# Head gates by seven block products, kept in DRAM; heads in two lanes; the second projection's weight sums all in layer 2

## The chip, the cores and the metric

The kernel runs on one core of a Trainium2 chip. Its time is the device time of one execution in microseconds (us). The kernel before was timed three times: 1390.17, 1392.6 and 1392.98 us, with a median of 1392.6 us. One more execution was profiled; the rows below come from it, and it took 1390.15 us.

## What is computed

512 tokens of width 2048 pass through two layers in float32. Layer 1 (cut from the reference):

```python
q, k, v, g_att, z, xbc, dt_raw = split(x @ w_in)       # q,k,v,g_att,z: 512 x 1024 each
o = rms_norm(diff_attention(q, k, v, lam), subln_g) * (1.0 - lam_init)   # 8 heads of 128
y_att = o.reshape(s, 1024) * silu(g_att)
y = ssd_chunked(...) + d_skip * xs                      # 16 state-space heads of 64
y = rms_norm(y * silu(z)) * ssm_norm_g                  # in two groups of 512
x = layer_norm(alpha * x + concat([y_att, y]) @ w_out)
```

Layer 2 projects x to a value and a gate path of 2048 each, pools the values over causal windows of 2, 4, 8 and 16 tokens in four groups, maps each group by a 512 x 512 matrix, multiplies by the gates, and sends that through a second output projection and a layer norm.

## The kernel before

**Products.** Each float32 product is three matmuls (`mm3`, L106 to L108): high part by high part, and the two cross terms. Weights come in "units" of 128 x 1024 float32 (512 KB). `unit` (L119) loads one by a DMA on SyncE's queue into a `raw` buffer (three in turn); ScalarE casts it to `hi` (L116), and VectorE subtracts to get `lo` (L117). A block of 128 output columns for all 512 tokens (`ws_block`) takes two units and 48 matmuls.

**Seven block products.** The z gate and both output projections are computed as 2 x 2 block matrices with seven block products in place of eight (`prod`, four units and 48 matmuls for one block product of z). This needs sums of weight blocks. `presum` (L240) makes them by DMA alone on GpSimd's queue: it copies blocks into an SBUF buffer, adds others by accumulating DMAs (L236), and writes each partial sum to DRAM (L238). Each step waits for the one before in its buffer. Two such chains (a pair) run at a time, in two lanes `sums2`. Layer 1 uses the buffers `pre` and `pre3`. In layer 2 each chain has a buffer `pre2` that shares its place (`h1` or `l1`) with a later tile: `yr2`, the third pooling group's result, takes `h1`, and `yr3` takes `l1`. GpSimd's queue also holds the small powers of the norms (`power`, L231), and it works strictly in order.

**Lanes.** A lane is a list of Python generators. Work with its own chain of waits is written as steps with `yield us`. Each `mm3` tells all lanes how much matmul time has been written since, and a lane whose wait is over writes its next step. So the order on TensorE is fixed when the program is built: small matmuls stand between large ones, and TensorE works through them in that order, waiting where an operand is late.

**Order of layer 1.** B, C, x and v projections with the state-space steps; the z gate; then for each head h `k_block`, `q_block` and `g_block` of the head before (48 matmuls each). `attention(h)` is pushed to `lane`: for each of four query blocks i `scores(i)` (into psc, with max, exp and the combination on VectorE and ScalarE), `turn(i)` (transposes into pat, copied to aT) and `values(i)` (into pav). After `values(3)` come four squares of pav on ScalarE (L706), two small VectorE operations, the power on GpSimd (L231) and the scaling `o` on VectorE (L712). Then `pot` transposes o (L719), and VectorE multiplies it by gain and gate into yTa (L722). After the heads follows the first output projection: Y = a11 by w (`pY`), which runs beside the last head's attention, then V (`pZ`), which needs yTa of all heads, then the products with sums.

**Layer 2.** For each group `vblock`, `pool_block`, `gblock` and the group map (`pgr`); VectorE forms y (L972), and ScalarE writes `yr` from it (L974). After the residual has been moved to DRAM (`x1d`, L916), three pairs of wo2 chains follow in GpSimd's queue; the first pair of all wo2 sums was made in layer 1.

Of the kernel before, what the change touches and what calls it, by code (L numbers as in the profile page):

```python
# [16 lines left out]
P = 128  # L17
T = 512
# [70 lines left out]
def hybrid_trunk(ctx: ExitStack, tc: tile.TileContext, xT, xtok, wa, wg, wz, wo1, wo2, prm, con, lnp, out, dbg=None):  # L89
# [135 lines left out]
    tsz, ts1, ts2 = {}, {}, {}  # L225
# [44 lines left out]
    with ExitStack() as l1:  # L270
# [14 lines left out]
        with ExitStack() as sd:  # L285
# [235 lines left out]
        with tc.tile_pool(name="zs", bufs=1) as zq:  # L521
# [46 lines left out]
            for i in range(2):  # L568
                c = zq.tile([P, T], F32, tag="zc", name="zc", bufs=2)
                nc.scalar.copy(c, Wz[i])  # L570
                nc.vector.tensor_tensor(c, c, Yz[i], ALU.add)
                th = zq.tile([P, 2, T], F32, tag="zo", name="zt", bufs=2)
                z_gate(2 + i, 0, c, th[:, 0])
                nc.vector.tensor_tensor(c22[i], c22[i], Yz[i], ALU.subtract)
                z_gate(2 + i, 1, c22[i], th[:, 1])
            for l in sums2:
                l.off = False
# [5 lines left out]
        ssq = at.tile([P, 8], F32, name="ssq")  # L583

        def ssm_norm(g):
# [11 lines left out]
            for c in range(4):  # L597
# [5 lines left out]
                yield 1.5  # L603

# [29 lines left out]

        gts = {}

        def g_block(h):
            pg = bank("mm", "pgt")
            ws_block(pg, next_units(2), xh, xl)
            gt = a2.tile([P, T], F32, tag="gt", name="gt")  # L640
            gate(gt, pg)
            gts[h] = gt

        def attention(h, kS, qH, qL):
# [32 lines left out]
            def values(i):  # L677
# [3 lines left out]
            yield 2.5  # L681
            scores(0)
            yield 3.5
            scores(1)
            yield 3.5
            turn(0)
            scores(2)
            pav = bank("aux", "pav")
            yield 2.5
            values(0)  # L690
            turn(1)
            yield 3.0
            values(1)
            scores(3)
            yield 2.5
            turn(2)
            yield 3.0
            values(2)
            yield 1.5
            turn(3)  # L700
            yield 3.0
            values(3)
            ss = a2.tile([P, 2, NT], F32, tag="ss", name="ss")
            for i in range(NT):
                junk = a2.tile([P, T], F32, tag="gth", name="junk")
                nc.scalar.activation(junk[:, :P], pav[:, ts(i)], AF.Square, accum_out=ss[:, 0, i:i + 1])  # L706
            s0 = st[:, 1, :, 0]
            nc.vector.scalar_tensor_tensor(ss[:, 1], in0=s0, scalar=EPS, in1=s0, op0=ALU.mult, op1=ALU.mult)
            nc.vector.scalar_tensor_tensor(ss[:, 0], in0=ss[:, 0], scalar=1.0 / P, in1=ss[:, 1], op0=ALU.mult, op1=ALU.add)
            power(ss[:, 0], 4)  # L710
            o = a2.tile([P, NT, P], F32, tag="o", name="o")
            nc.vector.tensor_tensor(o, pav.rearrange("p (i e) -> p i e", i=NT),  # L712
                                    ss[:, 0].unsqueeze(2).broadcast_to([P, NT, P]), ALU.mult)
            yield 5.5
            while h not in gts:
                yield 0.5
            pt = bank("aux", "pot")
            for i in range(NT):
                nc.tensor.transpose(pt[:, ts(i)], o[:, i], ident)  # L719
            if yTa[0] is None:  # L720
                yTa[0] = keep.tile([P, HEADS, T], F32, tag="y", name="yTa")
            nc.vector.scalar_tensor_tensor(yTa[0][:, h], in0=pt, scalar=subg, in1=gts[h], op0=ALU.mult, op1=ALU.mult)  # L722
# [41 lines left out]
        lane.flush()  # L764
        eight(a12, lambda u: yA[:, u:u + 2, H0], (6,))
# [107 lines left out]
    with ExitStack() as l2:  # L873
# [27 lines left out]
        with ExitStack() as mix:  # L901
# [18 lines left out]
            for g, w in enumerate(WINDOWS):  # L920
# [54 lines left out]
                if g == 0:  # L975
# [13 lines left out]
                    for i in range(2, 8):  # L989
                        sums2[i % 2].push(presum(wo2, ts2, i // 4, i % 4, stage2(i % 2), 10.0))  # L990
# [136 lines left out]
def _pack(inputs):  # L1127
# [17 lines left out]
    for h in range(HEADS):  # L1145
        ua += ws(w1, 1024 + P * h) + ws(w1, P * h)
        if h > 0:
            ua += ws(w1, 3072 + P * (h - 1))
    ua += ws(w1, 3072 + P * (HEADS - 1))
# [11 lines left out]
    sz = w1[:, 4096:5120].reshape(2, 4, 2, P, 1, 2, 512).transpose(4, 0, 5, 1, 3, 2, 6).reshape(16, P, 1024)  # L1161
# [27 lines left out]
    return {"xT": xT, "xtok": x.reshape(NT, P, D), "wa": wa, "wg": wg, "wz": sz, "wo1": so1, "wo2": so2, "prm": prm, "con": con, "lnp": lnp}  # L1189
# [18 lines left out]
```

## Time and profile before

| | |
|---|---|
| median of three runs | 1392.6 us (1390.17 to 1392.98) |
| profiled execution | 1390.15 us, span 1388.3 us |
| TensorE busy | 1372.6 us, 99% of the span, 6653 matmuls |
| VectorE, ScalarE, GpSimd busy | 870.9, 591.0, 189.1 us |
| mean granted TensorE clock | 0.997 |
| moved by DMA | 304.82 MB, mean 220 GB/s |

The time of the profiled execution is 1.85 us above its span. A share of busy time alone does not tell which engine sets the time; the waits and the rows of a stretch do. "TensorE busy" counts matmuls from start to modelled end, and they overlap, so durations of matmuls are read from the distance of their starts.

### The profile page before, as it was taken

The numbers are of one execution on the slowest core, as the hardware profiler recorded it, in microseconds if no ns is written. First come the engines' busy times: TensorE is split into PE (matmuls) and PEld (weight loads), VectorE is DVE, ScalarE is ACT, GpSimd is POOL, SyncE is SP. The second block draws the span as 40 slices with busy tenths as digits, with TensorE's granted clock in tenths as the row PEclk, the third lists the DMA queues.
The fourth block names the chain that finished last, engine by engine and source line by source line (L and its number), as shares of the span: only waits on it lengthen the run. The fifth ranks groups of instructions, "written<-read, shape, count | busy, mean of one in ns | idle before, by whom it ended". The sixth has DMA issues, their size and how long they took to land.

```text
span 1388.3 us, 17493 instructions
## 1 busy us (share of the span) xinstructions
PE 1372.6 (99%) x6653; PEld 1156.6 (83%) x6653; DVE 870.9 (63%) x1251; ACT 591.0 (43%) x960; POOL 189.1 (14%) x285
## 2 busy tenths in 40 slices
PE   9999999999999999999999999999999999999996
PEld 7988899888888888888888889888888888888875
DVE  7755764577645555556796897855345256466766
ACT  5232443456554444445544556333232232345443
POOL 0222220000221122200000000222221000200003
PEclk9999999999999999999999999999999999999998
DMA  8899996467777698832586556699999423566776
GB/s 303 270 313 303 276 265 182 123 238 247 244 198 232 198 265 245 239 123 76 174 294 193 176 179 189 220 319 293 311 289 289 135 91 95 181 202 195 246 247 122
DMA packets 88036, 304.82 MB, mean 220 GB/s; under 512 B 10000, under 2 KB 10128, under 8 KB 87568
## 3 DMA queue, kind: packets, MB, share of 16 engines
q1 hardware_dynamic: 52704, 177.86, 38.5%
q0 software_dynamic: 35248, 125.85, 33.5%
q8 instruction: 52, 0.85, 0.3%
q14 instruction: 32, 0.26, 0.1%
HBM read 249.14 MB, written 57.67 MB: 221 GB/s over the span
## 4 chain that ended last, share of the span: by engine, by line
PE 91%; DVE 4%; DMA 2%; issue 1%; ACT 1%; POOL 1%; DVEq 0%; ACTq 0%; POOLq 0%; SPq 0%
PE pg L106 6%; PE pg L107 6%; PE pg L108 6%; PE pY L107 4%; PE pY L108 4%; PE pY L106 4%; PE pv L107 4%; PE pv L106 4%; PE pv L108 4%; PE pZ L107 3%; PE pZ L106 3%; PE pZ L108 3%; PE pgt L108 2%; PE pxs L106 2%; PE pgt L106 2%; PE pxs L108 2%
## 5 line engine op out<-in xcount | busy, mean ns | idle before, releaser
L117 DVE TENSOR_TENSOR lo<-raw,hi 128x1024 fp32r<-128x1024 f32 (+3 forms) x314 | 373.5, 1190 | 326.3 <-ACT hi L116 323.3
L116 ACT CAST hi<-raw 128x1024 fp32r<-128x1024 f32 (+3 forms) x314 | 321.4, 1024 | 526.0 <-PE pY L108 83.6
L107 PE MATMUL pv<-x1l,hi 128*128 128x512 f32 (+1 forms) x320 | 110.9, 347 | 0.0
L106 PE MATMUL pv<-x1h,hi 128*128 128x512 f32 (+1 forms) x320 | 110.9, 347 | 0.0
L108 PE MATMUL pv<-x1h,lo 128*128 128x512 f32 (+1 forms) x320 | 110.7, 347 | 0.0
L106 PE MATMUL pg<-x1h,hi 128*128 128x512 f32 x256 | 99.6, 389 | 0.0
L107 PE MATMUL pg<-x1l,hi 128*128 128x512 f32 x256 | 99.6, 389 | 0.0
L108 PE MATMUL pg<-x1h,lo 128*128 128x512 f32 x256 | 99.6, 389 | 0.0
L238 POOL DMA_DIRECT2D t<-pre x80 | 44.7, 560 | 209.7 <-DMA pre<-in_wo 159.3
L236 POOL DMA_DIRECT2D pre<-in_wo x64 | 56.4, 956 | 96.1 <-DMA t<-pre 52.9
L107 PEld LDWEIGHTS pv<-x1l,hi 128*128 128x128 f32 x320 | 60.5, 189 | 7.6
L106 PEld LDWEIGHTS pv<-x1h,hi 128*128 128x128 f32 x320 | 60.5, 189 | 7.6
L108 PEld LDWEIGHTS pv<-x1h,lo 128*128 128x128 f32 x320 | 60.4, 189 | 7.5
L106 PE MATMUL pg<-hi,xh 128*128 128x346 f32 (+1 forms) x192 | 63.6, 332 | 0.0
L107 PE MATMUL pg<-lo,xh 128*128 128x346 f32 (+1 forms) x192 | 61.8, 322 | 0.0
L108 PE MATMUL pg<-hi,xl 128*128 128x346 f32 (+1 forms) x192 | 61.5, 320 | 0.0
L659 ACT ACTIVATE pm<-psc,st 128x128 f32<-128x128 f32 (+3 forms) x64 | 33.1, 523 | 61.0 <-DVE st L656 60.9
L108 PEld LDWEIGHTS pg<-x1h,lo 128*128 128x128 f32 x256 | 48.1, 188 | 10.0
L106 PEld LDWEIGHTS pg<-x1h,hi 128*128 128x128 f32 x256 | 48.1, 188 | 10.0
L107 PEld LDWEIGHTS pg<-x1l,hi 128*128 128x128 f32 x256 | 48.1, 188 | 9.9
L106 PE MATMUL pq<-xh,hi 128*128 128x512 f32 x128 | 51.9, 405 | 0.0
L106 PE MATMUL pgt<-xh,hi 128*128 128x512 f32 x128 | 51.8, 405 | 0.0
(366 smaller groups left out, 3259.8 us busy)
## 6 DMA issues: line engine op xcount, KB each, us to landing
raw<-in_wa SPq DMA_DIRECT2D x150, 512.0 KB, 5.0
pre<-in_wo POOLq DMA_DIRECT2D x96, 512.0 KB, 8.1
t<-pre POOLq DMA_DIRECT2D x80, 512.0 KB, 6.0
raw<-t SPq DMA_DIRECT2D x80, 512.0 KB, 4.2
raw<-in_wo SPq DMA_DIRECT2D x48, 512.0 KB, 3.7
pre<-in_wz POOLq DMA_DIRECT2D x24, 512.0 KB, 8.6
raw<-in_wz SPq DMA_DIRECT2D x12, 512.0 KB, 3.7
raw<-in_wg SPq DMA_DIRECT2D x16, 346.0 KB, 6.5
```

The costliest lines, as they stand in the source:

```text
L106: nc.tensor.matmul(o, sh, mh, start=start, stop=False, skip_group_check=more)
L107: nc.tensor.matmul(o, sh, ml, start=False, stop=False, skip_group_check=more)
L108: nc.tensor.matmul(o, sl, mh, start=False, stop=stop, skip_group_check=more)
L116: nc.scalar.copy(hi, src)
L117: nc.vector.tensor_tensor(lo, src, hi.bitcast(F32), ALU.subtract)
L236: nc.gpsimd.dma_start(dst, src, accum_op=ALU.add)
L238: nc.gpsimd.dma_start(dst, src)
L659: nc.scalar.activation(pm[:, m, :ke], pt[:, m, :ke], AF.Exp, bias=st[:, 0, i, m:m + 1], scale=1.0, accum_out=st[:, 1, i, m:m + 1])
```

## The change

- The 16 weight blocks of the heads' gates become an input of their own, `wga`. After z, 28 units and 336 matmuls compute the gates by seven block products, with four more chains in `presum`. `g_gate` writes each gate tile to a DRAM tensor `gd` by GpSimd's queue (8 writes of 256 KB).
- The eight `g_block`s (384 matmuls) go. Each head loads its gate from `gd` on SyncE's queue (`gt`) and multiplies o by it on VectorE before the transposes; ScalarE scales pot into yTa.
- Even heads go to `lane`, odd heads to `lane2`, so that two heads interleave. `busy` keeps the second from taking pav before the first has formed o. Steps are paced at 1.1 times their figures, for the last head at 0.6.
- In layer 1 the chains are wz 4, wga 4 and wo1 8, with shorter waits; the two wo2 chains go to layer 2, where four pairs now follow each other in place of three.

```diff
-            for w, tsum, n, pace in ((wz, tsz, 4, 7.0), (wo1, ts1, 8, 8.0), (wo2, ts2, 2, 8.0)):
+            for w, tsum, n, pace in ((wz, tsz, 4, 5.6), (wga, tsg, 4, 5.6), (wo1, ts1, 8, 6.0)):
...
+            def g_gate(t, j, c, th):
+                gate(th, c)
+                nc.gpsimd.dma_start(gd[:, t, j * 512:(j + 1) * 512], th)
...
+            gd = dram.tile([P, NT, 1024], F32, name="gd")
+            Yg = pair("mm")
+            for ch in range(4):
+                prod(Yg, xblock(0, H0), unit(wsrc(wga, 0, 0, 0, ch)), ch, True, False)
+            Wg = pair("sc")
+            for ch in range(4):
+                prod(Wg, z3, unit(tsg[3, 0, ch]), ch, True, False)
+            z1 = zsum("z1")
+            fill(z1, 1)
...
-        def g_block(h):
-            pg = bank("mm", "pgt")
-            ws_block(pg, next_units(2), xh, xl)
-            gt = a2.tile([P, T], F32, tag="gt", name="gt")
-            gate(gt, pg)
-            gts[h] = gt
...
+                while busy:
+                    yield 0.5
+                busy.append(h)
+                pav = bank("aux", "pav")
+                gt = a2.tile([P, NT, P], F32, tag="gt", name="gt")
+                nc.sync.dma_start(gt, gd[:, :, ts(h)])
...
+                nc.vector.tensor_tensor(o, o, gt, ALU.mult)
+                busy.remove(h)
+                yield 5.5
+                while len(normed) < 2:
+                    yield 0.5
+                pt = bank("aux", "pot")
...
+                nc.scalar.activation(yTa[0][:, h], pt, AF.Copy, scale=subg)
+
+            for us in steps():
+                yield us * (0.6 if h == HEADS - 1 else 1.1)
...
-            lane.push(attention(h, kS, qH, qL))
-            if h > 0:
-                g_block(h - 1)
-        g_block(HEADS - 1)
+            (lane, lane2)[h % 2].push(attention(h, kS, qH, qL))
...
         lane.flush()
+        lane2.flush()
...
-                    for i in range(2, 8):
-                        sums2[i % 2].push(presum(wo2, ts2, i // 4, i % 4, stage2(i % 2), 10.0))
+                    for i in range(8):
+                        sums2[i % 2].push(presum(wo2, ts2, i // 4, i % 4, stage2(i % 2), 8.0))
```

Three places in the order of instructions. The first is TensorE at the end of the last head's attention, beside the first output projection (pY). Before, from the last `values` (pav) to the first matmul of V (pZ), there are 24 matmuls of pY, of which the first and last rows stand here:

```order
L679 MATMUL pav<-v,aT 128x128 x4
L106 MATMUL pY<-hi,a11h 128x512
L107 MATMUL pY<-lo,a11h 128x512
...
L107 MATMUL pY<-lo,a11h 128x512
L108 MATMUL pY<-hi,a11l 128x512
L719 MATMUL pot<-kc,o 128x128 x4
L106 MATMUL pZ<-hi,a12h 128x512
```

And after the change, at the same place, with every row from pav to pZ:

```order
L728 MATMUL pav<-v,aT 128x128 x4
L106 MATMUL pY<-hi,a11h 128x512
L107 MATMUL pY<-lo,a11h 128x512
L108 MATMUL pY<-hi,a11l 128x512
L106 MATMUL pY<-hi,a11h 128x512
L107 MATMUL pY<-lo,a11h 128x512
L108 MATMUL pY<-hi,a11l 128x512
L106 MATMUL pY<-hi,a11h 128x512
L107 MATMUL pY<-lo,a11h 128x512
L108 MATMUL pY<-hi,a11l 128x512
L776 MATMUL pot<-kc,o 128x128 x4
L106 MATMUL pZ<-hi,a12h 128x512
```

Nine matmuls of pY are left between the last values and the transposes of o. The second place is the same head's scores of the last query block, a little earlier on TensorE. After the change it reads:

```order
L702 MATMUL psc<-kS,qH 128x512
L703 MATMUL psc<-kS,qL 128x512
L721 MATMUL pat<-kc,pm 128x128 x3
...
L776 MATMUL pot<-kc,o 128x128 x4
L728 MATMUL pav<-v,aT 128x128 x3
...
L107 MATMUL pY<-lo,a11h 128x512
L721 MATMUL pat<-kc,pm 128x128 x4
```

Between psc and the four transposes pat stand 14 matmuls of pY and three groups of small ones, one of them (pot) of head 6; before there were 33 matmuls of pY and two groups. The third place is GpSimd's queue in layer 2, at the end of the wo2 chains. Before, the last pair (buffers 9006 and 9009; t_12 and t_13 are sums in DRAM) ends like this, and the next row loads the residual:

```order
L236 DMA pre_9006<-in_wo 128x1024
L236 DMA pre_9009<-in_wo 128x1024
L238 DMA t_12_9235<-pre_9006 128x1024
L238 DMA t_13_9240<-pre_9009 128x1024
L1004 DMA xq_9977<-x1d 128x512 x4
```

After the change one more pair stands between the third and that row; it begins and ends like this:

```order
L238 DMA t_10_9278<-pre_8915 128x1024
L238 DMA t_11_9280<-pre_8918 128x1024
L238 DMA pre_9327<-in_wo 128x1024 x2
L238 DMA pre_9330<-in_wo 128x1024 x2
...
L238 DMA t_12_9378<-pre_9327 128x1024
L236 DMA pre_9330<-in_wo 128x1024
L238 DMA t_13_9390<-pre_9330 128x1024
L1062 DMA xq_10127<-x1d 128x512 x4
```

The pair's instructions are the same in kind and number (4 copies, 6 accumulations, 8 writes), and there is nothing else between the pairs.

## Rows read from the trace of the kernel before

**Rows 1.** The page: busy us and share of each engine, instructions.

```profile
PE 1372.6 (99%) x6653; PEld 1156.6 (83%) x6653; DVE 870.9 (63%) x1251; ACT 591.0 (43%) x960; POOL 189.1 (14%) x285
```

**Rows 2.** Waits (engine, line, waited for: total us, times, longest us).

```profile
PE pbc L306 <- DVE nhalf L174: 1.5, 1, 1.5
PE px L838 <- DVE xp L832: 0.7, 2, 0.5
```

**Rows 3.** Chain that ended last: pot of head 0 and of head 7.

```profile
409.82 0.44 PE pot L719 x4
...
685.00 0.44 PE pot L719 x4
```

**Rows 4.** Windows of z and of a head: us, PE, PEld, DVE, ACT, POOL, clock, DMA share, GB/s.

```profile
285.00:358.00 73.00, 72.85 (x322) 59.74 (x322) 54.25 (x60) 43.90 (x59) 0.78 (x1) 1.00 0.68 227
...
420.00:460.00 40.00, 40.00 (x198) 33.55 (x197) 21.29 (x39) 17.14 (x41) 7.89 (x12) 1.00 0.77 230
```

**Rows 5.** TensorE's timeline (start us, duration us): a k block and the q block behind.

```profile
343.37 0.39 PE L106 MATMUL pk<-xh,hi 128*128 128x512 f32 x1
...
354.25 0.39 PE L106 MATMUL pq<-xh,hi 128*128 128x512 f32 x1
```

**Rows 6.** Groups by form (busy us, mean ns of one | idle before): lo, and o.

```profile
L117 DVE TENSOR_TENSOR lo<-raw,hi 128x1024 fp32r<-128x1024 f32 x286 | 349.6, 1223 | 300.6 <-ACT hi L116 298.0 <-PE pseg L442 0.6
...
L712 DVE TENSOR_TENSOR o<-pav,ss 128x512 f32<-128x512 f32 x8 | 5.5, 692 | 9.6 <-POOL ss L231 9.6
```

**Rows 7.** Timeline of the last head's end, TensorE and VectorE.

```profile
678.49 1.06 PE L679 MATMUL pav<-v,aT 128*128 128x128 f32 x8
...
684.84 0.60 PE L719 MATMUL pot<-kc,o 128*128 128x128 f32 x4
...
682.25 0.69 DVE L712 TENSOR_TENSOR o<-pav,ss 128x512 f32<-128x512 f32 x1 [1.19 <-POOL ss L231]
```

**Rows 8.** Timeline of the last head's scores of query block 3.

```profile
666.46 0.39 PE L654 MATMUL psc<-kS,qL 128*128 128x512 f32 x1
...
675.29 0.60 PE L672 MATMUL pat<-kc,pm 128*128 128x128 f32 x4
...
671.89 0.75 DVE L664 SCALAR_TENSOR_TENSOR pm<-pm,st 128x512 f32<-128x512 f32 x1
```

**Rows 9.** GpSimd's timeline in layer 2: starts of the three pairs, last write from h1.

```profile
908.91 0.55 POOL L238 DMA_DIRECT2D pre<-in_wo  x1
...
973.93 1.06 POOL L238 DMA_DIRECT2D pre<-in_wo  x2 [1.46 <-DMA t<-pre]
...
1026.62 1.06 POOL L238 DMA_DIRECT2D pre<-in_wo  x2 [1.91 <-DMA t<-pre]
...
1073.22 0.56 POOL L238 DMA_DIRECT2D t<-pre  x1 [4.54 <-DMA pre<-in_wo]
```

**Rows 10.** DMA issues near 1026 (copy), 1065 (accumulation), 1073 us (write): KB, us to landing.

```profile
pre<-in_wo POOLq DMA_DIRECT2D x4, 512.0 KB, 6.4
...
pre<-in_wo POOLq DMA_DIRECT2D x1, 512.0 KB, 7.3
...
t<-pre POOLq DMA_DIRECT2D x1, 512.0 KB, 5.4
```

**Rows 11.** ScalarE's timeline in layer 2 around the first write of yr2.

```profile
1114.52 0.72 ACT L974 ACTIVATE yr<-y,osc 128x512 f32<-128x512 f32 x1 [2.19 <-DVE y L972]
1116.27 1.05 ACT L116 CAST hi<-raw 128x1024 fp32r<-128x1024 f32 x1 [1.03 <-PE pgr L107]
...
1127.10 1.05 ACT L116 CAST hi<-raw 128x1024 fp32r<-128x1024 f32 x1 [1.87 <-PE pv L107]
```

**Rows 12.** TensorE's first matmuls, and two windows at the end (columns as in rows 4).

```profile
1.46 3.95 PE L306 MATMUL pbc<-warm 128*128 128x512 f32 x9 [1.46 <-DVE nhalf L174]
...
1376.00:1380.00 4.00, 0.00 (x0) 0.00 (x0) 3.90 (x8) 0.00 (x0) 3.37 (x4) 1.00 1.03 115
1380.00:1384.00 4.00, 0.00 (x0) 0.00 (x0) 3.69 (x6) 0.00 (x0) 0.00 (x0) 0.57 1.03 213
```

More of the change, by code (lines that the diff above doesn't have):

```diff
@@ L88, in hybrid_trunk @@
 @with_exitstack
-def hybrid_trunk(ctx: ExitStack, tc: tile.TileContext, xT, xtok, wa, wg, wz, wo1, wo2, prm, con, lnp, out, dbg=None):
+def hybrid_trunk(ctx: ExitStack, tc: tile.TileContext, xT, xtok, wa, wg, wz, wga, wo1, wo2, prm, con, lnp, out, dbg=None):
     nc = tc.nc
@@ new lines, in hybrid_trunk @@
+            Wg = pair("sc")
[3 more added lines that the diff above has]
+            fill(z1, 1)
+            c22 = [zq.tile([P, T], F32, tag=f"c22{i}", name=f"g22{i}") for i in range(2)]
+            for i in range(2):
+                nc.scalar.activation(c22[i], Wg[i], AF.Copy, scale=-1.0)
+            Vg = pair("mm")
+            for ch in range(4):
+                prod(Vg, xblock(8, H0), unit(wsrc(wga, 1, 0, 0, ch)), ch, True, True)
@@ new lines, in hybrid_trunk @@
+            th = g_th()
+            for i in range(2):
+                c = zq.tile([P, T], F32, tag="zc", name="gc", bufs=2)
+                nc.scalar.copy(c, Vg[i])
+                nc.vector.tensor_tensor(c, c, Yg[i], ALU.add)
+                g_gate(i, 0, c, th[:, i])
+            for ch in range(4):
+                prod(Wg, xblock(8, H1), unit(tsg[4, 0, ch]), ch, False, True)
+            Zg = pair("mm")
+            for ch in range(4):
+                prod(Zg, z1, unit(tsg[1, 0, ch]), ch, True, False)
@@ new lines, in hybrid_trunk @@
+            for i in range(2):
+                nc.vector.tensor_tensor(c22[i], c22[i], Zg[i], ALU.add)
+            for ch in range(4):
+                prod(Yg, z2, unit(tsg[2, 0, ch]), ch, False, True)
+            for i in range(2):
+                th = g_th()
+                c = zq.tile([P, T], F32, tag="zc", name="gc", bufs=2)
+                nc.scalar.copy(c, Wg[i])
+                nc.vector.tensor_tensor(c, c, Yg[i], ALU.add)
+                g_gate(2 + i, 0, c, th[:, 0])
+                nc.vector.tensor_tensor(c22[i], c22[i], Yg[i], ALU.subtract)
+                g_gate(2 + i, 1, c22[i], th[:, 1])
@@ L576, in hybrid_trunk @@
+            for ch in range(4):
+                prod(Zg, z4, unit(wsrc(wga, 1, 1, 0, ch)), ch, False, True)
+            th = g_th()
+            for i in range(2):
+                c = zq.tile([P, T], F32, tag="zc", name="gc", bufs=2)
+                nc.scalar.activation(c, Yg[i], AF.Copy, scale=-1.0)
+                nc.vector.tensor_tensor(c, c, Zg[i], ALU.add)
+                g_gate(i, 1, c, th[:, i])
             for l in sums2:
@@ L583, in hybrid_trunk @@
         ssq = at.tile([P, 8], F32, name="ssq")
+        normed, busy = [], []
         def ssm_norm(g):
@@ L603, in ssm_norm @@
                 yield 1.5
+            normed.append(g)
         for g in range(2):
@@ L675, in turn, with values @@
                 pms[i] = aT
-            def values(i):
+            def values(i, pav):
                 for kb in range(i + 1):
                     nc.tensor.matmul(pav[:, ts(i)], pms[i][:, ts(kb)], v[:, kb, ts(h)], start=(kb == 0), stop=(kb == i))
[L681 to L713, printed above, removed]
@@ L1188, in _pack @@
     lnp = np.stack([f("ln_g"), f("ln_b")], axis=1)
-    return {"xT": xT, "xtok": x.reshape(NT, P, D), "wa": wa, "wg": wg, "wz": sz, "wo1": so1, "wo2": so2, "prm": prm, "con": con, "lnp": lnp}
+    return {"xT": xT, "xtok": x.reshape(NT, P, D), "wa": wa, "wg": wg, "wz": sz, "wga": sg, "wo1": so1, "wo2": so2, "prm": prm, "con": con, "lnp": lnp}
 def kernel(**inputs):
```

57 lines of the change are left out of this document (42 added, 15 removed).

## The prediction

> **What bounds the kernel now.** The page comes first: TensorE is busy for 1372.6 us of a span of 1388.3 [rows 1]. The waits then say whether it ever stands still for an operand: its two longest entries are 1.5 us at the start and 0.7 us in a norm [rows 2]. So the span is the length of what is written on TensorE, and a stretch gets shorter if matmuls leave it, as long as nothing that they hid comes to light. The chain of waits shows the same in the heads: pot of head 0 stands at 409.82 and that of head 7 at 685.00 [rows 3], seven heads at 39.3 us. Last come the windows, to see who has room. In z, VectorE is busy for 54.25 us of 73 and ScalarE for 43.90, while the DMA engines are busy to 0.68; in a head, VectorE has 21.29 us of 40 [rows 4].
>
> **Price of one matmul.** 48 matmuls of a k block lie between 343.37 and 354.25 [rows 5], 0.2267 us each. Durations of single matmuls (0.39 in the same rows) overlap and are not used.
>
> **What is removed.** The change takes out 384 gate matmuls and adds 336; the small ones stay as many. 48 fewer by 0.2267 give **-10.9 us**, if the seven products run without stalls and the shorter heads still cover attention.
>
> *The seven products.* A unit now feeds 12 matmuls (2.7 us) where a gate block's fed 24. The z stage works at just this rate until the first k block at 343.37 [rows 5], and the window that is mostly z has TensorE at 72.85 of 73 us [rows 4]. The added stage is the same code with the same splits, and it has less elementwise work than z (no product with y). Its eight gate writes leave on GpSimd's queue, and the first reader comes a head later. I take 0.
>
> *The heads.* A head had 144 large matmuls, 32.6 us, in a period of 39.3; so 6.7 us are small ones. With 96 the period is 21.8 + 6.7 = 28.5 us. VectorE had about 21 us of work in a head and loses the splits of two units, the gate and the last product, and gains one multiply of 0.69 (as o, [rows 6]); even 21 us would be under three quarters of 28.5. The steps of one head ask for 31 us, times 1.1 is 34.1, and one head's 32 calls of `mm3` tick 32 x 3 x 512/2400 = 20.5. One lane would fall behind by 13.6 a head; two lanes have 41. So the interleaving is needed, and it is enough on paper. The gate load and the pot copy on ScalarE stand where nobody queues behind them for long: 0.
>
> **What comes to light: the end of attention.** V needs the last head, and before, 24 matmuls (5.4 us) of pY stood between its last pav and pot. After the change there are nine, 2.04 us. What must happen in between is read from the trace: pav ends at 678.49 + 1.06 = 679.55, o ends at 682.25 + 0.69 = 682.94 [rows 7], 3.4 us for squares, power and scaling. The new multiply adds 0.69, a hand-over some 0.1: 4.2 - 2.04 = 2.2 us of waiting. A little earlier, 14 matmuls and three small groups, some 4.3 us, separate the last psc from its transposes, where there were 33 and two. The chain of max, exp and combination took from 666.85 (psc's end) to 672.64 (pm's end) [rows 8], 5.8 us. Against 4.3 that is a wait of 1.5; it is 0 if the work of VectorE and ScalarE for the projection that stood among it stands elsewhere. I take 0.8, the middle. Together **+3** (2 to 5.5, the upper end if two splits of 1.2 us [rows 6] also fall into its chain). TensorE has nothing else to do: pZ stands behind pot in its order.
>
> **What comes to light: layer 2.** yr2 lies in h1, the buffer of the even chains. Before, the last write from h1 started at 1073.22 [rows 9] and landed after 5.4 [rows 10], at 1078.6, long before yr2's first write at 1114.52 [rows 11]. Now a fourth chain begins in h1 at 1078.6. How long? Between bounds: the sum of its own landings is 6.4 + 3 x 7.3 + 3 x 5.4 = 44.5 us [rows 10]; the second and third pair took 52.7 (973.93 to 1026.62) and 52.0 [rows 9], the queue's waits for the other chain included. In the new order the even chain's last write stands ahead of the odd chain's last two steps, so I take 48: h1 is free at R = 1126.6 (1123 to 1131). ScalarE is in order, so the cast that ran at 1116.27 stands behind yr2's write until R. Three buffers are in turn and a unit lasts 5.4 us, so this cast fills the unit that TensorE takes up three units on, at 1127.1 (where the cast of 1127.10 finds pv's buffer freed, [rows 11]). It is ready at R + 0.72 (yr) + 1.05 (cast, [rows 11]) + 1.2 (lo, [rows 6]) = R + 3.0, and TensorE waits R - 1124.1, or 2.5 us; with the queue of casts and y behind it I take **+3** (0 to 8).
>
> *In layer 1* the two wo2 chains leave GpSimd's queue, and four wga chains come in. Two wz, two wga and four wo1 pairs of some 52 us [rows 9] now reach into the heads: four wo1 pairs are 208 us beside 228 us of heads. A power of a head's norm can stand behind an accumulation that waits up to 7.3 us; pot follows o's steps after 5.5 x 1.1 us of ticks, which is 6.6 us of matmuls and more, so nearly all is hidden. For this, the chain's last write before the buffers become `sr`, and denser DMA in z I take **+1.5** (0 to 4).
>
> **The sum.** -10.9 + 3 + 3 + 1.5 = -3.4 us. Against the profiled execution that is 1390.15 - 3.4 = 1386.8. That execution is as fast as the fastest of the three shown and 2.45 us under their median; against the median it gives 1389.2, and I say **1389.0**. All terms at their good ends give -8.9, at their bad ends +6.6.
>
> **Rivals.**
> 1. *All is hidden.* If pace 0.6 already lets the last head end early enough and the fourth chain needs only its own landings, -10.9 + 1 leaves 1382.7. For it speaks that TensorE hardly waits anywhere now [rows 2]; against it the nine matmuls against 4.2 us. 0.13.
> 2. *The gain is paid back in full.* The tail at 5.5 and layer 2 at 4 give -10.9 + 9.5 + 1.5 = 0.1, that is 1392.7. For it: every hidden chain was covered by the matmuls that leave. Against: two ends of ranges at once. 0.25.
> 3. *Slower: the fourth chain comes late.* Its place is yr2's first write in ScalarE's order. From R = 1130.5 on the change gains nothing, from 1133 it is slower by 0.2%. At R = 1136 the wait is 12 us, and -10.9 + 3 + 12 + 1.5 = +5.6 gives 1398. For it: the first pair took 65 us (908.91 to 973.93, [rows 9]), which would put R at 1143.6. Against: that pair began right behind the residual's move, the other two did not. 0.15.
> 4. *The heads do not get shorter,* because two heads' steps meet in the single pair of score banks or the lock on pav; 2 us a head bring 16, +12 in all, 1405. Against: VectorE's share and the 41 for 34 ticks. 0.03.
> 5. *The two waits bring TensorE's clock down.* The nine matmuls at the start took 3.95 us where nine at 0.2267 are 2.04 [rows 12], so a return from the lower level costs some 1.9 us; two of them make the sum +0.4, or 1393.0. Against it: at the kernel's end, with no matmul in either window, the granted clock still shows 1.00 from 1376 to 1380, and 0.57 only in the four us behind [rows 12]. My waits are of 3 us at most. In rival 3 it would add another 1.9. 0.04.
>
> The Trainium skill ("TensorE: Matmul & The Clock Gate", section "Why this matters for your kernels") has this as a rule: no idle gaps of TensorE between bursts of matmuls, since the clock falls back to half. The rows at the end show the fall, behind a longer stop than my waits.
>
> **How the numbers follow.** The forecast has 0.40. A measurement of this kernel tells about 0.2%, 2.8 us, from no change. Faster by more are rival 1, some 0.33 of the forecast and 0.01 of rival 2: 0.47. Within it are 0.07 of the forecast, 0.24 of rival 2, 0.01 of rival 3 and rival 5: 0.36. Slower are the rest of rival 3 and rival 4: 0.17. The range runs from rival 1 (1383) to just short of rival 3 (1397); outside are half of rival 1, most of rival 3's late landings, and rival 4, about 2 in 10. The forecast alone would have 1385 to 1392.
>
> **What would show it.** TensorE should have 6605 matmuls. In the waits, pot on o (L776) should show some 2 us and pat on pm up to 1.5, both once, in the last head; a pgr or pv matmul behind yr2 should wait some 3 us on lo, and ScalarE's yr write should name a DMA of `t<-pre` as what it waited for. From pot to pot the heads should average 28.5 us. The prediction is wrong if waits stand in the middle heads or in the gate products, if the fourth pair takes 60 us, or if none of the waits is there.

## The result, and the profile after

The changed kernel takes 1398.45 us (median of 20 runs, 1393.45 to 1405.03); the kernel before, run beside it, takes 1391.2 (1389.8 to 1393.53). The ratio is 1.0055, with a 95% interval of 1.0046 to 1.0064: slower by 0.55%, where 0.2% faster was forecast. The time lies just above the range, near that of rival 3. The profiled execution has a span of 1396.2 us against 1388.3.

First the waits of the kernel after: TensorE's own, those of VectorE and ScalarE that matter (engine, line, waited for: total us, times, longest).

```profile
PE pv L106 <- ACT hi L116: 5.0, 1, 5.0
PE pat L721 <- ACT yTa L779: 2.6, 2, 2.1
PE pot L776 <- DVE o L769: 2.1, 1, 2.1
...
PE pat L721 <- DVE pm L713: 0.5, 1, 0.5
...
DVE o L767 <- POOL ss L231: 12.2, 8, 3.3
...
ACT yr L1032 <- DMA t<-pre: 18.2, 1, 18.2
```

Five waits of TensorE of 0.5 to 5 us have joined those of [rows 2]: one in layer 2 behind yr2, two in middle heads (pat on yTa, 2.1 and 0.5), and two in the last head. The matmuls are 6605, as expected.

Where along the kernel was the time lost? Two places in TensorE's timeline tell: the first matmul of V behind the heads, and the last matmul. Before, V began right behind pot [rows 7]:

```profile
685.19 0.48 PE L106 MATMUL pZ<-hi,a12h 128*128 128x512 f32 x1
...
1375.16 0.39 PE L108 MATMUL pZ<-wl,cl 128*128 128x512 f32 x1
```

After, from the same view:

```profile
685.05 0.63 PE L776 MATMUL pot<-kc,o 128*128 128x128 f32 x4 [2.11 <-DVE o L769]
685.44 0.48 PE L106 MATMUL pZ<-hi,a12h 128*128 128x512 f32 x1
...
1383.07 0.39 PE L108 MATMUL pZ<-wl,cl 128*128 128x512 f32 x1
```

At V the kernel with 48 matmuls fewer is level with the old one (+0.25 us): all of the 10.9 us has been given back in layer 1 already. Its last matmul is at 1383.07 where that of the kernel before was at 1375.16, +7.9 us; so some 7.7 us come after V. The chain of waits after the change, with start, duration and what, shows them at one place in layer 2:

```profile
1121.82 5.67 DMA pre<-in_wo
...
1127.79 2.90 DMA t<-pre
...
1130.95 0.06 ACT yr L1032
...
1131.58 1.04 ACT hi L116
...
1132.65 0.80 PE pv L106
...
1134.71 0.43 PE pv L106
...
1138.37 0.23 PE pv L106
```

The last write of sums from h1 lands at 1130.7; yr2's first write follows at once, behind it the cast that stood in ScalarE's queue, and then TensorE, which had run out of units after 1127.5. That is 5.1 us by the distance of the matmuls. Behind it the matmuls stand 0.43 us apart instead of 0.23, and only from 1138.1 on at the old pitch: TensorE runs at half clock. The windows say the same (us, PE, PEld, DVE, ACT, POOL busy, granted clock, DMA share, GB/s), here and around the wait in the middle head at 495.84:

```profile
494.00:498.00 4.00, 2.16 (x7) 1.81 (x8) 2.23 (x4) 3.00 (x7) 0.57 (x1) 0.79 0.95 228
498.00:502.00 4.00, 4.00 (x17) 3.37 (x16) 1.02 (x2) 0.00 (x0) 1.12 (x2) 0.78 1.01 349
1126.00:1130.00 4.00, 1.70 (x8) 1.08 (x6) 0.00 (x0) 0.00 (x0) 1.23 (x2) 1.00 0.76 275
1130.00:1134.00 4.00, 1.31 (x3) 0.59 (x3) 1.36 (x2) 2.28 (x3) 0.20 (x1) 0.65 0.82 149
1134.00:1138.00 4.00, 4.00 (x10) 3.13 (x11) 2.56 (x4) 2.94 (x4) 0.55 (x1) 0.50 0.77 253
```

The trace's record of the granted clock has 6.8 us at 0.5 in layer 2 (1131.2 to 1138.0) and 3.4 us in the head (496.3 to 499.8). A stretch of 6.8 us at half speed holds 3.4 us of work; some of it was still waiting, and counted by the distance of the matmuls it cost 2.9 us, in the head 1.8. So layer 2 lost 5.1 + 2.9 = 8.0 us.

And the middle head? In these rows of the timelines of GpSimd, VectorE, ScalarE and TensorE the wait at 495.84 is traced back:

```profile
486.25 0.53 POOL L238 DMA_DIRECT2D t<-pre  x1 [3.12 <-DMA pre<-in_wo]
486.80 1.04 POOL L231 TENSOR_TENSOR ss<-ss,nhalf 128x4 f32<-128x4 f32 x1
...
484.44 0.15 DVE L764 SCALAR_TENSOR_TENSOR ss<-ss 128x4 f32<-128x4 f32 x1
487.87 0.69 DVE L767 TENSOR_TENSOR o<-pav,ss 128x512 f32<-128x512 f32 x1 [3.28 <-POOL ss L231]
...
492.92 0.96 DVE L705 TENSOR_REDUCE st<-psc 128x2 f32<-128x768 f32 x1
...
493.97 0.58 ACT L708 ACTIVATE pm<-psc,st 128x384 f32<-128x384 f32 x1 [4.77 <-DVE st L705]
...
495.10 0.69 ACT L779 ACTIVATE yTa<-pot,subg 128x512 f32<-128x512 f32 x1
...
491.07 0.60 PE L776 MATMUL pot<-kc,o 128*128 128x128 f32 x4
...
495.84 0.44 PE L721 MATMUL pat<-kc,pm 128*128 128x128 f32 x2 [2.11 <-ACT yTa L779]
```

VectorE had the mean squares ready at 484.6, but the power stands in GpSimd's queue behind a write of sums that waits for its accumulation to land, and runs at 486.80. VectorE waits in order at o (3.28 us). Behind o stand a split, two parts of kS and the maximum of the *other* head's scores, which comes at 492.92. ScalarE waits for it with the exponentials (4.77 us), and behind these, in its order, stands the copy of pot to yTa, though pot has been done since 491.7. Only two of the small PSUM banks (`aux`) exist; one is the other head's pav, one is pot. So pat of the other head, which needs a bank, waits until 495.8 for that copy.

### The profile page after: what moved, and what is told of

The parts are those of the page before. It is cut to its first block, busy times and chain, and to the rows that moved or that the text cites. A ratio compares the mean times of both kernels' runs of the same rounds, so it can differ in the third digit from the quotient of the medians.

```text
span 1396.2 us, 17592 instructions
## 1 busy us (share of the span) xinstructions
PE 1370.2 (98%) x6605; PEld 1148.7 (82%) x6605; DVE 892.9 (64%) x1275; ACT 613.5 (44%) x990; POOL 220.3 (16%) x333
## 4 chain that ended last, share of the span: by engine, by line
PE 69%; DMA 19%; DVE 4%; issue 4%; POOL 2%; ACT 1%; DVEq 0%; POOLq 0%; ACTq 0%; SPq 0%
DMA pre<-in_wo 11%; DMA t<-pre 6%; PE pY L107 6%; PE pY L106 6%; PE pY L108 6%; PE pg L106 4%; PE pg L107 4%; PE pg L108 4%; PE pZ L107 3%; PE pZ L106 3%; PE pZ L108 3%; PE pxs L106 2%; PE pxs L108 2%; PE pxs L107 2%; PE pv L108 2%
## 5 line engine op out<-in xcount | busy, mean ns | idle before, releaser
L117 DVE TENSOR_TENSOR lo<-raw,hi 128x1024 fp32r<-128x1024 f32 (+3 forms) x326 | 388.3, 1192 | 300.8 <-ACT hi L116 297.2
L116 ACT CAST hi<-raw 128x1024 fp32r<-128x1024 f32 (+3 forms) x326 | 334.3, 1025 | 477.3 <-PE pY L108 94.9
L238 POOL DMA_DIRECT2D t<-pre x96 | 54.4, 567 | 251.1 <-DMA pre<-in_wo 155.4
L108 PEld LDWEIGHTS pg<-x1h,lo 128*128 128x128 f32 x256 | 48.1, 188 | 10.3 <-DVE lo L117 0.4
L106 PE MATMUL pxs<-xh,hi 128*128 128x512 f32 x128 | 51.7, 404 | 0.0
L106 PE MATMUL pk<-xh,hi 128*128 128x512 f32 x128 | 51.3, 401 | 0.0
```

The costliest lines, as they stand in the source:

```text
L106: nc.tensor.matmul(o, sh, mh, start=start, stop=False, skip_group_check=more)
L108: nc.tensor.matmul(o, sl, mh, start=False, stop=stop, skip_group_check=more)
L116: nc.scalar.copy(hi, src)
L117: nc.vector.tensor_tensor(lo, src, hi.bitcast(F32), ALU.subtract)
L238: nc.gpsimd.dma_start(dst, src)
```

## Experiments

Each kernel here was timed beside the kernel before, whose median was 1390.8 to 1391.8 us; the ratios are against it. The changed kernel was not timed again with them, so a difference from its 1398.45 us is good to some 0.6 us, besides its own spread.

**The move of the chains alone.** In the kernel before:

```diff
-            for w, tsum, n, pace in (... (wo1, ts1, 8, 8.0), (wo2, ts2, 2, 8.0)):
+            for w, tsum, n, pace in (... (wo1, ts1, 8, 8.0)):
...
-                    for i in range(2, 8):
-                        sums2[i % 2].push(presum(..., 10.0))
+                    for i in range(8):
+                        sums2[i % 2].push(presum(..., 8.0))
```

> The kernel before, with only the chains of the second projection moved: none in layer 1, four pairs in layer 2 as in the change. Theory (the fourth pair holds yr2's buffer and so ScalarE's queue, and TensorE stands still and then runs for some us at the lower clock level): one wait of about 5 us at a pv matmul on a cast, a stretch of about 7 us at granted clock 0.5 behind it, and +8 us on the kernel before (+4 to +12). Rival (the cost comes from two-lane heads and gates, and layer 2 only looks bad because it starts late there): no wait in layer 2, 0 to +2 us.

It took 1401.78 us, ratio 1.0077 (1.0059 to 1.0096): the kernel before gets 10 us slower by this part alone. But the place was only partly the expected one. Layer 2 has its wait, ScalarE at yr for 14.8 us, but TensorE loses only 1.6 us there in the profiled execution, with no stretch at half clock. The larger loss is a new one in the heads: of the 11.5 us by which its last matmul comes later than before, some 6 lie in the heads, 3.0 in layer 2, and the rest ahead of the heads. The rows (waits, then TensorE's timeline):

```profile
PE pv L106 <- ACT hi L116: 1.6, 1, 1.6
...
DVE sr L759 <- DMA t<-pre: 5.4, 1, 5.4
...
540.78 0.58 PE L653 MATMUL psc<-kS,qH 128*128 128x256 f32 x1 [3.47 <-ACT pm L659]
```

`sr` takes over the chains' buffer for the first projection's differences. With the last chain of layer 1 ending sooner, the scheduler puts this VectorE operation earlier in order, in the middle of a head, and there it waits 5.4 us for the chain's last write (it runs at 538.5; in the kernel before, `sr` first ran at 607.1). From 539.4 on the clock is at half for 6.8 us. So the theory holds for the sign, and for the wait behind the shared buffer; that the size came out near its 8 us is luck, since most of it is from elsewhere. A chain's end has a second reader, whose place in VectorE's order also counts.

**Without the fourth pair in layer 2.** The changed kernel with plain weight blocks in place of the first pair's eight sums; the chains for i = 0 and 1 are left out.

> The changed kernel, with the first pair of the second projection's sums left out (plain weight blocks stand in for its eight sums), so that three pairs are left in layer 2. Theory: yr2's wait and the half-clock stretch in layer 2 are gone, 7.9 us less than the changed kernel, about 1390.5 us, which is the kernel before within 2 us. Rival (layer 2's wait is one of several symptoms of denser DMA traffic): less than 4 us less.

It took 1391.86 us, ratio 1.0005 (0.9994 to 1.0016), 6.6 us under the changed kernel. The wait in layer 2 and the half clock are gone. So this is what makes the change slower; what is left is no slower than before, and no faster. In the profiled execution the middle head waits as long as in the changed kernel, and yet keeps its clock:

```profile
497.17 0.44 PE L721 MATMUL pat<-kc,pm 128*128 128x128 f32 x2 [2.12 <-ACT yTa L779]
...
492.00:496.00 4.00, 3.05 (x17) 2.23 (x15) 3.10 (x5) 0.70 (x3) 1.11 (x2) 1.00 0.94 149
496.00:500.00 4.00, 2.83 (x16) 2.45 (x17) 2.23 (x4) 2.32 (x5) 0.57 (x1) 1.00 1.05 255
```

**All work, but no sharing of h1.** The even chains' long-lived buffer gets 4 KB of its own; the room comes from the residual's two vectors, which move into h1.

```diff
                             a = lp.tile([P, 2, 1024], F32, tag=("h1", "l1")[n], name="pre2")
+                            if n == 0:
+                                return lp.tile([P, 1024], F32, tag="pa", name="pre2t"), a[:, 1]
                             return a[:, 0], a[:, 1]
...
-                    ab = [p2.tile([P, T], F32, tag=f"ab{i}", ...) for i in range(2)]
+                    ab = [abt[:, 2 * (cg % 2) + i] for i in range(2)]
```

> The changed kernel with all its work, but the even chains' long-lived buffer in a place of its own (4 KB a partition, won from the residual's two vectors, which move into h1), so that only the short-lived t3 lies in h1, which yr2 takes. Theory (the sharing of h1, not the DMA traffic, is what layer 2 pays for): no wait of ScalarE on a write of sums at yr2, no wait of TensorE there, no stretch at half clock in layer 2; about 1391.9 us, as with the fourth pair left out (1390 to 1394), 6.6 us less than the changed kernel. Rival (four chains beside layer 2's loads cost by themselves): still 3 us or more over the kernel with the fourth pair left out.

It took 1394.7 us, ratio 1.0028 (1.0019 to 1.0038): 3.7 us under the changed kernel, not 6.6. yr2's wait is gone, four pairs or not. But the edit did more than it was meant to, since the residual's vectors now lie in a place that is free sooner. First, the residual's move ends sooner, and the chains, which stand behind it in GpSimd's queue, begin 21.8 us sooner. GpSimd's timeline has the first copy of the changed kernel, and then the first copy and the even chains' last write of this one:

```profile
911.53 1.60 POOL L238 DMA_DIRECT2D pre<-in_wo  x3
```

```profile
889.77 0.55 POOL L238 DMA_DIRECT2D pre2t<-in_wo  x1
...
1108.67 0.56 POOL L238 DMA_DIRECT2D t<-pre2t  x1 [2.57 <-DMA pre2t<-in_wo]
```

That write lands 5.1 us later, at 1113.8. In the changed kernel ScalarE came to yr2's first write at 1112.7 (18.2 us before 1130.95), and TensorE ran out of work only after 1127.5. So a shared buffer would have been free in time as well, and this run does not separate its own place from the earlier start; that yr2 waits for the chain's write stands in the changed kernel's rows alone (ACT yr <- DMA t<-pre). Second, the scheduler puts the residual's VectorE work ahead of the norm's at the start of layer 2, and transposes (px) wait 1.4 us for ScalarE's z. The rival's "3 us or more over" (2.8 by the medians) nearly came true in the number, but hardly by its cause: layer 2 is 1.8 us longer than without the fourth pair in the profiled executions, of which the norm's stop is 1.4, and the heads are 1.6 us longer, where here the clock was at half from 496.9 to 500.3.

**The chains in the gate stage.** They run during the gates' seven products too, and the first wo2 pair stays in layer 1.

```diff
+            for l in sums2:
+                l.off = False
             gd = dram.tile([P, NT, 1024], F32, name="gd")
...
-            ... (wo1, ts1, 8, 6.0)):
+            ... (wo1, ts1, 8, 6.0), (wo2, ts2, 2, 6.0)):
...
-                    for i in range(8):
+                    for i in range(2, 8):
```

> The changed kernel, with the chains let run during the gates' seven products too, the first pair of the second projection's sums made in layer 1 behind those of the first, and three pairs in layer 2. Theory: layer 2 loses its wait and its half-clock stretch, -7.9; the chains in the gate stage cost nothing that shows; the power's waits in the heads remain in some form (-2 to +2): about 1390.5 us (1388 to 1393). Rival (DMA traffic is what costs: unit loads of 512 KB every 2.7 us and chains together): the gate stage gets waits on weight units of more than 5 us in all, and little is won.

It took 1427.2 us, ratio 1.0259 (1.0245 to 1.0272). Here the rival is right. Nothing else stands in GpSimd's queue during z, and these chains already run there (its rows are busy for 12.96 us in the window below, and not at all in the changed kernel's). The window from z into the gate stage, first of this kernel and then of the changed one, and the DMA issues of the same stretch (290 to 360 us, in the same order):

```profile
290.00:360.00 70.00, 58.62 (x224) 43.93 (x223) 36.71 (x36) 29.69 (x34) 12.96 (x19) 0.93 1.03 338
...
raw<-t SPq DMA_DIRECT2D x11, 512.0 KB, 9.7
```

```profile
290.00:360.00 70.00, 69.77 (x307) 57.17 (x306) 55.34 (x59) 42.08 (x49) 0.00 (x0) 1.00 0.76 254
...
raw<-t SPq DMA_DIRECT2D x15, 512.0 KB, 4.4
```

A unit takes 9.7 us to land instead of 4.4 while TensorE uses one up every 2.7 us, and TensorE does 224 matmuls in place of 307. So the pause of the chains in the stages of seven products is needed at this pace of the loads. The change makes that pause as long again, and the chains it displaces are what collides with the heads and with yr2.

**The power left out.** Changed kernel, o scaled by the mean square itself.

```diff
                 nc.vector.scalar_tensor_tensor(ss[:, 0], ...)
-                power(ss[:, 0], 4)
                 o = a2.tile([P, NT, P], F32, tag="o", name="o")
```

> The changed kernel, with the power of the heads' norms left out (o is scaled by the mean square itself), so that o no longer waits for GpSimd's queue. Theory (a head's power waits behind a chain's DMA in that queue, VectorE waits for it in order, the next head's scores come late, TensorE stands 2.1 us and the clock falls): the 2.1 us wait near 496 us and the half-clock stretch behind it are gone, and the last head's wait for o falls from 2.1 us to about 1; 4 to 6 us less than the changed kernel, about 1393.5 us; layer 2 stays as it is. Rival (the heads wait because VectorE and ScalarE are too full with two heads): the wait near 496 us stays, at most 1.5 us less.

It took 1440.35 us, ratio 1.0356: it tells little, since it changed the order too. `sr` came into VectorE's order in the middle of the heads and waited 50.9 us for a chain's last write. The wait near 496 is gone and that of the last pot fell from 2.1 to 0.9, as expected; the time can't be used.

**The multiplies swapped.** First pav by the gate, then by the power's result.

```diff
-                nc.vector.tensor_tensor(o, pav..., ss[:, 0]..., ALU.mult)
-                nc.vector.tensor_tensor(o, o, gt, ALU.mult)
+                nc.vector.tensor_tensor(o, pav..., gt, ALU.mult)
+                nc.vector.tensor_tensor(o, o, ss[:, 0]..., ALU.mult)
```

> The changed kernel with the two multiplies of o in the other order: first pav by the gate, which does not need the power, then by the power's result. Theory (the new multiply stands in the chain behind the power): the last head's wait for o falls from 2.1 to 1.4 us, the wait near 496 us by some 0.7 us too; 0.7 to 2 us less than the changed kernel, 1396.5 to 1397.8. Rival (the tail is set by something else, such as the squares on ScalarE or the transposes): the wait stays at 2.1, no change.

It took 1399.32 us, ratio 1.0051 (1.0035 to 1.0067): no gain. The tail did what theory says, 1.4 instead of 2.1. But the middle head waited longer, since the power was held longer by GpSimd's queue in this execution (waits, then VectorE's timeline):

```profile
PE pat L721 <- ACT yTa L778: 4.9, 2, 3.8
...
PE pot L775 <- DVE o L768: 1.4, 1, 1.4
...
490.43 0.69 DVE L768 TENSOR_TENSOR o<-o,ss 128x512 f32<-128x512 f32 x1 [5.05 <-POOL ss L231]
```

**The late multiply.** Swapped as above, and in all heads but the last the second multiply stands on VectorE behind the other head's next maximum (`lastred` is the last such instruction).

```diff
+                if h < HEADS - 1:
+                    yield 4.5
+                with tc.issue_after(lastred[0].ins) if h < HEADS - 1 else nullcontext():
+                    nc.vector.tensor_tensor(o, o, ss[:, 0]..., ALU.mult)
-                yield 5.5
+                yield 5.5 if h == HEADS - 1 else 2.0
```

> The changed kernel with the multiplies swapped and, in all heads but the last, the multiply by the power's result placed on VectorE behind the other head's next maximum (and pot some 1 us of ticks later), so that VectorE does not stand in order behind a power that is held in GpSimd's queue. Theory (a power behind a chain's DMA blocks VectorE, which delays the other head's scores): the wait of 2.1 us near 496 us and that of 0.5 near 555 are gone; with the tail's 0.7, 3 to 5 us less than the changed kernel, about 1394.5. Rival (VectorE and ScalarE are too full with two heads at once): the waits stay or move, under 1.5 us less.

It took 1394.01 us, ratio 1.0014 (1.0005 to 1.0023): 4.4 us under the changed kernel. VectorE's wait for the power falls from 12.2 us in eight times to one of 0.6, the waits near 496 and 555 are gone, and V starts at 680.45 instead of 685.44:

```profile
DVE o L773 <- POOL ss L232: 0.6, 1, 0.6
...
680.45 0.48 PE L106 MATMUL pZ<-hi,a12h 128*128 128x512 f32 x1
```

The same work is done, so full engines were not the cause. But this kernel also has pot a little later, and with it the order on TensorE changed: pat of the other head now stands ahead of pot. Which of the two it was is told by the next two.

**Pot later, nothing else.** VectorE stays as in the changed kernel; TensorE's order in the middle heads is that of the kernel with the late multiply.

```diff
-                yield 5.5
+                yield 5.5 if h == HEADS - 1 else 6.5
                 while len(normed) < 2:
```

> The changed kernel with one edit: in all heads but the last pot comes 1.1 us of ticks later (6.5 in place of 5.5), which puts the other head's transposes pat ahead of pot on TensorE, as in the kernel with the late multiply. VectorE keeps its order, so it still stands at o behind the power. Theory A (the bank: pat waits for the one of two small banks that pot holds until ScalarE has copied it, which stands in ScalarE's order behind the delayed exponentials): the wait of 2.1 us near 496 is gone, 3 to 5 us less than the changed kernel, as with the late multiply, while VectorE's waits at o stay at some 12 us. Theory B (what counts is that VectorE is blocked and the scores come late): the wait near 496 stays or moves to the next scores, under 1.5 us less.

It took 1395.02 us, ratio 1.0035 (1.0023 to 1.0047). VectorE waits for the power as long as before, and yet V starts as early as with the late multiply:

```profile
DVE o L767 <- POOL ss L231: 12.0, 8, 3.1
...
680.15 0.49 PE L106 MATMUL pZ<-hi,a12h 128*128 128x512 f32 x1
```

No wait of more than 0.2 us is left between 480 and 560 us. So it is theory A: in these heads the late power costs TensorE nothing as long as no transposes wait for pot's bank, and it was the order that helped, not the late multiply. The whole is 0.2% above the kernel with the late multiply, and the two intervals only touch. The profiled execution has two differences that can make it: the last pot waits 2.1 us instead of 1.4, as the swap is missing, and behind it the clock was at half from 680.6 to 684.0, which cost 1.7 us and did not happen there.

**Pot's copy back on VectorE.**

```diff
-                nc.scalar.activation(yTa[0][:, h], pt, AF.Copy, scale=subg)
+                nc.vector.tensor_scalar(yTa[0][:, h], pt, subg, None, op0=ALU.mult)
```

> The changed kernel with pot's copy into yTa back on VectorE (a multiply by the gain), the places on TensorE as in the changed kernel. On VectorE it comes right behind the other head's maximum, ahead of the exponentials that it waits for on ScalarE. Theory A (the bank that pot holds): the wait near 496 shrinks from 2.1 to about 1 us, since the copy ends about 1.2 us sooner; 1 to 3 us less than the changed kernel, clock included. Theory B: no change, since the scores are as late as before.

It took 1400.16 us, ratio 1.0064 (1.0048 to 1.008). In the heads it does what theory A says: the copy is freed from the exponentials, the wait is 0.7 instead of 2.1, and V starts at 683.63, 1.8 us sooner than in the changed kernel. The rows are of TensorE's timeline and waits:

```profile
494.66 0.44 PE L721 MATMUL pat<-kc,pm 128*128 128x128 f32 x2 [0.69 <-DVE yTa L779]
...
PE pv L106 <- ACT hi L116: 8.9, 1, 8.9
```

The whole is no faster, against theory A's 1 to 3 us: in this execution the last pot waited 3.3 us, and layer 2 8.9, with 10.2 us at half clock that began within that wait (1129.0 to 1139.2). The chains' last write from h1 landed at 1133.5 there, against 1130.7, and the first pair took 69.7 us up to the next one's start, in place of 65.8; why it did was not settled.

**Both remedies.**

> The changed kernel with both remedies: the even chains' own buffer, and the late multiply. Theory: the gains add up, -6.6 and -4: about 1388 us (1386 to 1390), 3 us less than the kernel before. Rival (waits taken away in the heads turn up elsewhere): 1391 or more, no better than the kernel before.

It took 1389.57 us, ratio 0.9983 (0.9974 to 0.9991). The gains add up (3.7 and 4.4 us under the changed kernel alone, 8.9 together), and the norm's wait that the residual's new place had brought is still there; here the clock fell behind it:

```profile
843.70 0.66 PE L899 MATMUL px<-kc,xp 128*128 128x128 f32 x4 [1.38 <-ACT z L905]
...
844.00:848.00 4.00, 3.71 (x18) 3.17 (x17) 4.00 (x8) 3.16 (x7) 0.73 (x2) 0.60 0.96 251
```

**Both, and the residual behind the norm.** `lastln` is VectorE's last instruction of the norm.

```diff
+                        with tc.issue_after(lastln[0].ins):
+                            nc.vector.scalar_tensor_tensor(xs, in0=xs, scalar=ALPHA, in1=ab[0], ...)
```

> Both remedies, and the residual's VectorE work in layer 2 placed behind the first layer's norm, as in the changed kernel (in the kernel with both remedies it had moved ahead, since its vectors then lie in a buffer that is free sooner, and a norm's transposes waited 1.4 us, with 3.4 us at half clock behind). Theory: that wait and the half-clock stretch go, some 3 us less than with both remedies: about 1386.5 us (1385 to 1389), 5 us less than the kernel before. Rival (the wait there is chance and moves): 1389 to 1390, as with both remedies.

It took 1385.85 us, ratio 0.9966 (0.9954 to 0.9978): this version beats both kernels, by 0.34% the one before. In its waits the longest of TensorE's is the start's, and of the waits at pot, pat and yr2 two at pot are left, 1.4 us in the last head and 0.6 in head 5:

```profile
PE pot L780 <- DVE o L774: 2.0, 2, 1.4
PE pbc L308 <- DVE nhalf L174: 1.5, 1, 1.5
```

Its runs lie within 1384.6 to 1387.64; the changed kernel's spread over 11.6 us.

**One lane.** The changed kernel with all heads in `lane`, all steps paced at 0.62.

```diff
-            (lane, lane2)[h % 2].push(attention(h, kS, qH, qL))
+            lane.push(attention(h, kS, qH, qL))
```

> The changed kernel with all heads in one lane, steps paced at 0.62 so that one head's steps (31 x 0.62 = 19.2) fit into its 20.5 us of ticks. Theory (with a head's period cut from 39.3 to 28.5 us, two heads must interleave): every head gets waits of TensorE on the scores' chain, some 2 to 5 us a head, 15 to 40 us over the changed kernel. Rival (the lanes do not matter, VectorE and ScalarE hold 28 us a head either way): within 5 us of the changed kernel.

It took 1417.43 us, ratio 1.0191 (1.0177 to 1.0205), 19 us over the changed kernel. Seven of eight heads wait at pot (10.3 us), one pat for 5.1, and the clock falls behind them. At this pace the second lane is needed once the gate blocks no longer fill the heads.

## Why the prediction was wrong, point by point

- **What is removed, -10.9 us.** Right. 6605 matmuls, and the seven products of the gates run without a stall worth naming (62.00 of 62 us busy from 358 to 420).
- **The end of attention, +3.** Nearly right in size: 3.4 by the distances of the matmuls, of which pot's wait on o is 2.1 as the sum had it (2.2). The 0.8 for the scores stood elsewhere than the sum said, 0.3 us ahead of the first scores (652.37) and 0.5 at the transposes of query block 1 (669.84); those of block 3 waited 0.2. That the multiply stands in this chain is shown by the swap (2.1 to 1.4).
- **Layer 2, +3.** The mechanism was right, the term mis-sized: 5.1 us of wait and 2.9 of half clock. The end of the chain was put at 1126.6 and was 1130.7. Not the fourth pair was the error (45.5 us, from 1085.44 to 1130.95; 48 were taken), but its start: 1078.6 was taken from the trace before, and it was 1085.4, since the first pair began 2.6 us later and the three pairs together took another 4 longer. In the other direction, the wait followed R by less than the sum said: only `hi` is needed for the first matmuls, not `lo`.
- **The half clock, rival 5, chance 0.04.** This was the step that failed most: the sum gave the clock nothing. The rows at the end of the kernel were read as if a stop of 3 us were safe, but they show one stop of one execution and bound no other. Behind stops of 2.1 and 5.0 us the clock fell, at a cost of 1.8 and 2.9 us (1.9 a fall was said), 4.7 of the 11.3 us between the sum (-3.4) and the span (+7.9). The rule of the Trainium skill that was cited there ("TensorE: Matmul & The Clock Gate", "Why this matters for your kernels") agrees with the fall behind 5.0 us. The one behind 2.1 us came after a shorter gap than that row of the page speaks of; there the measurement decides.
- **"The gate load and the pot copy on ScalarE stand where nobody queues behind them for long: 0."** Wrong. The copy frees the bank that the other head's pat takes next, and in ScalarE's order it stands behind exponentials that may be late. The sum gave nothing for it; it is 2.3 us near 496 and 0.7 near 555 by the distances of the matmuls, and the 1.8 us of clock on top. Putting pat ahead of pot takes it away.
- **Layer 1's small terms, +1.5.** What was said of the power in GpSimd's queue, that pot is late enough to hide it, is true of pot. What it delays is the other head's maximum on VectorE, and by that the copy; without the bank it is hidden, as the run with pot later shows.
- **The heads' period, 28.5 us.** 29.06 was measured: pot of two heads apart stands at 524.85 and 582.98. But the 0.7 us near 555 lie between these two, and are counted above. With pot later, where no such wait is left, it is 28.73 (521.00 to 578.46). So the sum was short by 0.2 us a head, some 2 us in all, which is in no wait. It is not that TensorE switches more often: from small to large matmuls it goes 18 times in two heads, and 20 times before. What it is, no run here separates. (The steps of a head ask for 30.5 us, not 31; nothing hangs on it.)

In sum: -10.9, +3.4 (tail), +4.8 (pot's bank and the clock in the heads), some +3 (period and what is left), +8.0 (layer 2) make +8.3 against 7.9 measured on the spans. Of the 11.3 us by which the sum was off, 4.7 are the clock, 3.0 the bank, 2.1 layer 2's wait, 0.4 the tail, and the 1.1 left the small terms. That the time meets rival 3's 1398 us is chance: rival 3 had the last write land at 1136 and TensorE wait 12 us; it landed at 1130.7, and TensorE waited 5.1. The forecast's sign hung on a margin of 3.4 us, and every term that took from it came in at or above its value.

What stays open: why the chains of layer 2 ran slower, and why their end, and with it layer 2's wait, differs by some us from kernel to kernel (1.6 to 8.9 us of TensorE's) though their instructions are the same. That they began 2.6 us later is told in part: they stand behind the residual's last move to DRAM, which began at 909.4 in place of 906.8, though layer 2's first matmul (pv) came only 0.2 us later (820.43 against 820.27). Open is also which of the two took the wait of layer 2 away in the last kernels, the even chains' own place or the earlier start of the chains.

## What to carry to other kernels

Here stalls of 2.1 and 5.0 us of TensorE cost another 1.8 and 2.9 us in clock, so a change that wins matmuls and pays in waits must be priced with both. When work is taken out of a saturated stage, list what it covered: here DMA chains lost their window, and reappeared behind a shared buffer and ahead of a norm's power. An instruction that moves to another engine takes along the release of what it reads: look at who takes that bank next, and at what the instruction now stands behind; placing one group of transposes ahead of another brought the start of V 5 us forward.

## What the hardware showed that was not expected

Waits of about the same length do not have the same price. A stop of TensorE of 2.11 us was followed by 3.4 us at 0.5 of the clock at 495.84 in the changed kernel; 2.12 us at the same place without the fourth pair, and 2.11 at the last pot, were not, and neither was the 3.27 at the last pot with the copy on VectorE. After 1.38 us in the norm the clock fell once, and after as long a wait there in the kernel with the own buffer alone it did not:

```profile
846.00:850.00 4.00, 2.42 (x19) 1.98 (x18) 3.81 (x7) 2.80 (x6) 1.60 (x3) 1.00 0.80 185
850.00:854.00 4.00, 3.78 (x31) 3.57 (x32) 4.00 (x9) 2.46 (x6) 0.54 (x1) 1.00 0.94 256
```

That one and the same kernel loses more clock in one execution than in another is told by its 20 runs: their mean granted clocks go from 0.996 to 0.989, and the times with them, from 1393.98 us at 0.996 to 1405.03 at 0.989. The runs of the kernel before, timed beside the experiments, all have 0.996 or 0.997, and so have all of the version with both remedies and the residual behind the norm. That goes some way to explain a spread of 11.6 us where the kernel before has 3.7; how much of it is the landing of the chains is not separated.
